# Row factors of two mixing stages spread over partitions through DRAM in place of TensorE transposes, with the planner's ranks set anew

## The chip, the cores and the metric

One core of one Trainium2 chip. The metric is the device time of one execution of the kernel in microseconds, the median of several runs; lower is better.

## The reference

One encoder layer is applied to two independent streams (`x_prompt` and `x_sample`), each 512 tokens of width 1024, everything in float32:

```python
x = x + 0.5 * swiglu(rms_norm(x, ffn1_norm), ...)            # 1024 -> 2816 -> 1024
h = rms_norm(x, mix_norm);  proj = h @ w_in                   # q, k, v, memory q/k/v, gates
att = gqa_block_attention(rope(rms_norm(q)), rope(rms_norm(k)), v)   # 8 heads of 64, softmax over 512 keys
mem = mlstm_bidirectional(...)                                # 4 heads of 128, forward and backward
merged = sigmoid(g_att) * (att @ w_up_att) + sigmoid(g_mlstm) * (mem @ w_up_mlstm)
x = x + merged @ w_out
x = x + 0.5 * swiglu(rms_norm(x, ffn2_norm), ...)
return rms_norm(x, final_norm)
```

Two per-token factors matter here. In the attention each head's output is divided by the sum of its softmax row:

```python
p = softmax(s);  o = p @ v            # the kernel: o = (exp(s - max) @ v) / sum
```

In the memory each head's output is normed over its 128 channels and gated:

```python
h = h * rsqrt(mean(h * h, -1) + EPS) * head_norm
out = sigmoid(o_pre) * h
```

## The kernel before

Activations lie channel-major: 128 channels on the partitions, 512 tokens along the free axis. Matrix products run as pairs of rounded and remaining parts (a weight and an activation are each split into a high and a low part, ACT copies the high part, DVE subtracts it), so a product of 128 channels takes three matmuls of 128x128x512. The two feed-forward parts (to about 640 us, and from about 1440 us) are straight loops. Between them lies the mixing of both streams, and it is the part that is changed.

The mixing isn't written in the order in which it runs. `mix(s, ...)` hands tasks to one planner (class `Plan`), for stream 0 and stream 1 and for parts of what stands before and behind them. Each task has an engine (PE is TensorE, DVE VectorE, ACT ScalarE, SP the queue that issues transfers), a modelled duration, tasks that it depends on, buffers that it takes and frees (`need`, `free`), and a rank. `run()` keeps a modelled clock for each engine and takes, of the tasks that could start at the earliest time, the one with the least rank. The order found so is the order of the instructions on each engine; nothing is reordered on the chip. A product has the base rank 5 (`FILL`), so products that nothing waits for fill gaps of others. The table `RANK` adds a number to the rank of named tasks, "part of the mixing, stream, engine, function"; its entries were found by search. The helper `dma` counts 0.35 us of SP for each transfer, and its landing after the bytes at 400 KB per us and 1.9 us more.

The stages that the change touches, per stream `s`:

- **Attention (`attend`)**. For each head and block of 128 queries, `scores` (two products), `peak` (DVE), `exp` (ACT, which also adds up the row's sum into column `i` of the small tile `tot`, 128 tokens on the partitions x 4 blocks x 2 heads). Then for each block of keys four transposes (`turn`, line 1275), a split (`high` on ACT, `lower` on DVE, line 1284) and `attend` (two products). `copy_o` and `add_o` bring the head's output into one half of the partitions of a tile `af`: two heads of 64 channels fill 128 partitions. The sums lie with tokens on the partitions but are needed along the free axis, repeated over the 64 channels of each head. For that, `recip` takes reciprocals, `spread` (ACT, line 1320) copies them 64 times side by side, `turn_r` (line 1327) turns the result by four 128x128 transposes into a PSUM bank, and `divide` (line 1331) multiplies. A split then writes the `att` tile, which `up_att` (the projection with `w_up_att`) reads. Before it comes `values`, the products that make the memory's values.
- **Memory (`memory`)**, four heads. The head's output stands in a PSUM bank. `squares` (line 1552), four transposes `sums_` (line 1561) and `reduced` make the sum of squares for each token, `rooted` the reciprocal root in eleven small DVE instructions (lines 154 to 172), `cast` spreads it over all partitions by four transposes of a repeated column (`bcast_psum`, line 188), and `ended` (line 1574) multiplies the gated output by it. A split (lines 814 and 817) writes the `mem` tile, which `up_mem` (the projection with `w_up_mlstm`) reads; its products for channel group k depend on head k, four groups to an output bank, nine products for the first three heads and three for the last. Three banks (`mm`) are there for it.

Buffers that play a part: `f2`, two slots of 128 x 2 x 512 numbers, used by `copy_o`, `add_o` (the tile `af`), the first gate of the memory and rows of the output projection; `pt`, two PSUM banks for all transposes; `wr`, four buffers for fetched weights (`fetch_w`, line 198), which ACT (line 830) and DVE (line 833) split.

`bcast_psum` is also used twice in the first feed-forward part (8 of its 40 transposes), which the change doesn't touch.

Of the kernel before, what the change touches and what calls it, by code (L numbers as in the profile page):

```python
# [26 lines left out]
def encoder(ctx, tc, I, outs):  # L27
# [49 lines left out]
    def wide(tag):  # L77
        return tpool.tile([P, 2, S], F32, tag=tag, bufs={"t2": 6, "f2": 2}[tag], name=nm(tag))
# [44 lines left out]
    def PT():  # L123
        return pt.tile([P, S], F32, tag="t", name=nm("pst"))
# [12 lines left out]
    def A(shape, dtype=F32, name="a"):  # L137
        return apool.tile(shape, dtype, tag="a", name=nm(name))
# [45 lines left out]
    def bcast_psum(r, pin=lambda i: i):  # L184

        pr = PT()
        for b in range(4):
            pin(nc.tensor.transpose(pr[:, b * P:(b + 1) * P], r[:, b:b + 1].to_broadcast([P, P]), ident))
        return pr
# [487 lines left out]
    def tok_proj(xh, xl, name, N, kk, done):  # L677
# [6 lines left out]
        def comp(k0, w):  # L684
# [14 lines left out]

    outs_of = []  # L700

    RANK = {"gsums ACT <lambda>": 5, "kv0 ACT raw": 0.5, "kv0 ACT gate": 2.5, "q0 SP w_fetch": -20,
            "rotate0 DVE by_cos": 4, "rotate0 DVE low": 5.5, "mem_qk0 SP w_fetch": -1.5, "mem_qk0 ACT w_high": -8.5,
            "mem_qk0 DVE w_low": 12, "out_gate0 SP w_fetch": -11, "attend0 ACT exp": -3, "attend0 PE turn": -15,
            "attend0 ACT copy_o": 13, "attend0 DVE s_low": 1, "maxima0 DVE masked": 7, "maxima0 DVE peak": 3,
            "maxima0 PE ends": -3, "maxima0 DVE scales": -1, "values0 PE fn": -68, "up_att0 ACT w_high": 14.5,
            "up_att0 PE fn": -2, "memory0 ACT one": 14.5, "memory0 DVE fn": -5, "memory0 PE turn": -1.5,
            "memory0 PE cast": 3.5, "memory0 DVE s_low": 3.5, "up_mem0 DVE w_low": -17, "up_mem0 DVE add": 7,
            "up_mem0 DVE s_low": 0.5, "after0 ACT high": -8, "kv1 ACT w_high": -6, "q1 ACT w_high": -0.5,
            "keys1 ACT copy_k": 18, "rotate1 DVE by_root": 43, "mem_qk1 ACT w_high": 13.5, "mem_qk1 ACT high": 6,  # L710
            "mem_qk1 DVE <lambda>": -6.5, "out_gate1 ACT w_high": -6, "attend1 PE scores": -2.18,
            "attend1 PE turn": -2, "attend1 PE turn_r": -1, "maxima1 DVE peak": -12.5, "values1 PE fn": -11,
            "up_att1 SP w_fetch": 10.5, "up_att1 ACT w_high": 51, "up_att1 PE fn": 9, "up_att1 DVE <lambda>": -15,
            "memory1 DVE masked": 3, "memory1 ACT one": 19, "memory1 ACT high": 27, "memory1 DVE gated": 0.68,
            "memory1 DVE rooted": 9.5, "before1 DVE <lambda>": 13, "up_mem1 PE fn": 13.5, "up_mem1 ACT s_high": 4.5}

    class Plan:

# [77 lines left out]
    def pe(n, width, fn, deps=(), pri=1, need=(), free=()):  # L796
        step = {512: 0.227, 128: 0.109, 16: 0.112}[width]
        return do("PE", n * step, (n - 1) * step + 0.35 + SPARE, fn, deps, pri, need, free)

    def act(w, fn, deps=(), pri=1, need=(), free=(), more=0.0):  # L800
        return do("ACT", ACT_STEP[w] + more, ACT_STEP[w] + 0.12 + more + SPARE, fn, deps, pri, need, free)

    def dve(w, fn, deps=(), pri=1, need=(), free=(), n=1):
        return do("DVE", n * DVE_STEP[w], n * DVE_STEP[w] + 0.08 + SPARE, fn, deps, pri, need, free)
# [16 lines left out]
    def weights(view, deps=(), need=(), w=1024):  # L821
# [15 lines left out]
        t2 = dve(w, w_low, [t1], 2, (), ["wr"])  # L837
        return c, t2

    def unit(c, ready, n, cols, src, done, last=True, each=None):  # L840

        b = {}
        t = None
        for k in range(n):
            for i in range(3):
                def fn(k=k, i=i):
                    if k == 0 and i == 0:
                        b["p"] = MM()
                    sh, sl = src(k)
                    w_, x_ = ((c["hi"], sh), (c["hi"], sl), (c["lo"], sh))[i]  # L850
                    own(nc.tensor.matmul(b["p"], w_[:, k, cols], x_, start=(k == 0 and i == 0),  # L851
                                         stop=(k == n - 1 and i == 2)))
                first, end = k == 0 and i == 0, k == n - 1 and i == 2
                new = [each[k]] if each and i == 0 else []
                t = do("PE", 0.227, 0.35 + SPARE if end else 0.0, fn, new + ([t] if t else ready), FILL, ["mm"] if first else (),
                       ["w"] if end and last else ())
        done(b, t)
        return t

# [33 lines left out]
    def mix(s, before, after, x_in, start, got, more=None):  # L893
# [352 lines left out]
        for h in range(HA):  # L1246
# [66 lines left out]
            if h % 2:  # L1313
                i = h // 2

                def recip(i=i):
                    own(V_.reciprocal(G["tot", i], G["tot", i]))

                def spread(i=i):
                    own(nc.scalar.activation(G["af", i][:, 1].rearrange("p (b i e) -> p b i e", i=2, e=DA),  # L1320
                                             G["tot", i].unsqueeze(3).to_broadcast([P, 4, 2, DA]), AF.Copy))

                def turn_r(i=i):
                    pr = G["rp", i] = PT()
                    for b in range(4):
                        bs = slice(b * P, (b + 1) * P)
                        own(nc.tensor.transpose(pr[:, bs], G["af", i][:, 1, bs], ident))

                def divide(i=i):
                    af = G["af", i][:, 0]  # L1330
                    own(V_.tensor_tensor(af, af, G["rp", i], op=ALU.mult))
                u = dve(8, recip, [exps[g, b] for g in (h - 1, h) for b in range(4)], 1)
                u = act(512, spread, [u, adds[h - 1]], 1)
                u = pe(4, 128, turn_r, [u, last_a[h]], 0, ["pt"])
                u = dve(512, divide, [u, adds[h - 1], adds[h]], 0, (), ["pt"])
                att_in.append(split_of(lambda i=i: G["af", i][:, 0], lambda i=i: att()[:, i, 0, :],
                                       lambda i=i: att()[:, i, 1, :], [u, att_t], 1, free=["f2"]))

# [91 lines left out]
        for h in range(HM):  # L1430
# [136 lines left out]
            def rooted(h=h):  # L1567
                G["rh", h] = rstd_cols(G["cs", h], 4, DM, own)

            def cast(h=h):  # L1570
                G["Rp", h] = bcast_psum(G["rh", h], own)

            def ended(h=h):
                own(V_.scalar_tensor_tensor(ogs[h], ogs[h], hn[:, h:h + 1], G["Rp", h], op0=ALU.mult, op1=ALU.mult))
            sq_ = act(512, squares, [prev], 0, ["turn"])
            gt_ = dve(512, gated, [prev, og_in[h], sq_], 1, (), [bank])
            u = pe(4, 128, sums_, [sq_], 0, ["pt"], ["turn"])
            u = dve(512, reduced, [u], 0, (), ["pt"])
            u = dve(8, rooted, [u], 0, n=20)
            u = pe(4, 128, cast, [u], 0, ["pt"])  # L1580
            u = dve(512, ended, [u, gt_], 0, (), ["pt"])
            mem_in.append(split_of(lambda h=h: ogs[h], lambda h=h: mem()[:, h, 0, :], lambda h=h: mem()[:, h, 1, :],
                                   [u, mem_t], 1))

# [43 lines left out]
        if s:  # L1628
            do.part = f"last{s}"
            swap(w3, ["qk", "qk"], ["w", "w"])  # L1630
            rows, into = {}, [None, None]
            rows_t = do("POOL", 0.0, 0.0, lambda: rows.update(t=A([P, 2, 4, S], F32, "rows")), [mh_t], 0, ["A"])
            ends = []

            def out_last(h):
                def fetch():
                    nc.sync.dma_start(rows["t"][:, h], xbuf[1][:, h])
                into[h] = dma(fetch, [rows_t], 3, kb=1024)

                def done(bk, q, t):  # L1640
                    x = lambda: rows["t"][:, h, q, :]

                    def add():
                        own(V_.scalar_tensor_tensor(x(), bk[q], 0.5, x(), op0=ALU.mult, op1=ALU.add))

                    def sq():
                        own(nc.scalar.activation(bk[q], x(), AF.Square, accum_out=ssq2[1][:, h, q:q + 1]))
                    u = dve(512, add, [t, into[h]], 1)
                    ends.append(act(512, sq, [u], 1, (), [bank_of(q)], more=0.2))
                    dma(lambda: nc.sync.dma_start(x2buf[1][:, h, q, :], x()), [u], 2, kb=256)  # L1650
                return token_blocks([wov[h, j] for j in range(4)], lambda k: (mhl["h"][:, k, :], mhl["l"][:, k, :]), 512, done, [last_w], ended)
            out_t = [out_last(h) for h in range(2)][1]
            swap([out_t], (), ["A", "A"])
            return rows, ends, turned
# [36 lines left out]
    rbuf = [[dpool.tile([P, 7, 2, S], F32, name=f"rbuf{n}_{j}") for j in range(NF // 2)] for n in range(2)]  # L1691
    xnbuf, xn1buf = [dpool.tile([P, KD, S], F32, name=n) for n in ("xnbuf", "xn1buf")]
    gbuf = [[dpool.tile([P, KD, S], F32, name=f"gbuf{s}_{i}") for i in range(2)] for s in range(2)]
    gated_in = [[[], []], [[], []]]
    xc = [None] * 7
    up = Up(xc, I["ffn1_w_gate"], I["ffn1_w_up"], rbuf[0], AHEAD[0])
# [913 lines left out]
```

## Time and profile before

| | |
|---|---|
| median of three runs | 2040.72 us (2040.3 to 2041.28) |
| span of the profiled execution, first to last instruction | 2039.6 us |
| what the runs' median has beyond that span | 1.1 us |
| PE busy | 2021.7 us (99%) |
| DVE busy | 1597.7 us (78%) |
| ACT busy | 965.5 us (47%) |
| granted TensorE clock | 0.999 |

The page gives no time of the profiled execution but its span. Busy times are unions over the span. A group of instructions has a row with its line, engine, operation, tiles and shape, its count, its busy time, the mean duration of one, and the engine's idle time just before it. Matmuls are pipelined: one with 512 columns is recorded as 389 ns long, but the next can start well before that has passed, so the cost of one more is read from start to start. `PEld` is the load of weights, which runs beside products; `SPq` the queue that issues transfers.

### The profile page before, as it was taken

The numbers are of one execution on the slowest core, as the hardware profiler recorded it, in microseconds if no ns is written. First come the engines' busy times: TensorE is split into PE (matmuls) and PEld (weight loads), VectorE is DVE, ScalarE is ACT, GpSimd is POOL, SyncE is SP. The second block draws the span as 40 slices with busy tenths as digits, with TensorE's granted clock in tenths as the row PEclk, the third lists the DMA queues.
The fourth block names the chain that finished last, engine by engine and source line by source line (L and its number), as shares of the span: only waits on it lengthen the run. The fifth ranks groups of instructions, "written<-read, shape, count | busy, mean of one in ns | idle before, by whom it ended". The sixth has DMA issues, their size and how long they took to land.

```text
span 2039.6 us, 26019 instructions
## 1 busy us (share of the span) xinstructions
PE 2021.7 (99%) x9308; PEld 1671.2 (82%) x9308; DVE 1597.7 (78%) x2532; ACT 965.5 (47%) x1604; POOL 23.9 (1%) x49
## 2 busy tenths in 40 slices
PE   9999999999999999999999999999999999999997
PEld 8888888888888888877888888888788888888886
DVE  7997878786796764897888866876888787776687
ACT  7543434342227533587645775656443344343224
POOL 0000000000000000000000000000000000000001
PEclk9999999999999999999999999999999999999999
DMA  9556555799774645312345322464464644389753
GB/s 347 179 174 218 181 191 203 245 363 358 249 252 155 217 150 177 104 42 85 125 133 166 123 83 73 165 208 151 138 230 168 212 173 147 135 303 394 269 201 143
DMA packets 149633, 389.02 MB, mean 191 GB/s; under 512 B 15232, under 2 KB 15296, under 8 KB 147712
## 3 DMA queue, kind: packets, MB, share of 16 engines
q1 hardware_dynamic: 148640, 385.33, 54.5%
q8 instruction: 73, 1.20, 0.2%
q0 software_dynamic: 432, 1.25, 0.2%
q10 hardware_dynamic: 432, 0.79, 0.1%
q14 instruction: 56, 0.46, 0.1%
HBM read 269.31 MB, written 118.00 MB: 190 GB/s over the span
## 4 chain that ended last, share of the span: by engine, by line
PE 89%; DVE 6%; ACT 2%; DMA 1%; issue 1%; SPq 0%; DVEq 0%; ACTq 0%
PE pss L292 17%; PE pst L292 11%; PE mm L851 9%; PE mm L292 8%; PE mm L553 8%; PE mm L881 7%; PE pst L553 4%; PE pss L553 4%; PE pss L2151 3%; PE pso L553 3%; PE mm L2151 2%; PE pso L881 2%; PE pst L2151 2%; PE pst L1275 1%; PE pss L1251 1%
## 5 line engine op out<-in xcount | busy, mean ns | idle before, releaser
L292 PE MATMUL pss<-xc,w 128*128 128x512 f32 x1632 | 389.4, 389 | 1.0 <-ACT w L247 0.6
L292 PEld LDWEIGHTS pss<-xc,w 128*128 128x128 f32 x1632 | 305.9, 188 | 66.2 <-ACT w L247 1.0
L247 ACT ACTIVATE w<-wr 128x1024 fp32r<-128x1024 f32 (+2 forms) x123 | 127.4, 1038 | 219.6 <-PE pst L292 122.9
L248 DVE TENSOR_TENSOR w<-wr,w 128x1024 fp32r<-128x1024 f32 (+2 forms) x123 | 146.9, 1196 | 59.0 <-ACT w L247 58.7
L292 PE MATMUL mm<-xc,w 128*128 128x512 f32 x792 | 190.4, 390 | 0.1
L553 PE MATMUL mm<-w,rt 128*128 128x512 f32 x792 | 185.3, 389 | 0.0
L292 PEld LDWEIGHTS mm<-xc,w 128*128 128x128 f32 x792 | 148.3, 188 | 31.9 <-ACT t L301 0.6
L553 PEld LDWEIGHTS mm<-w,rt 128*128 128x128 f32 x792 | 148.5, 188 | 30.8
L292 PE MATMUL pst<-xc,w 128*128 128x512 f32 x528 | 127.0, 389 | 0.0
L292 PE MATMUL pst<-xc,f 128*128 128x512 f32 x528 | 126.8, 389 | 0.0
L833 DVE TENSOR_TENSOR w<-wr,w 128x1024 fp32r<-128x1024 f32 (+1 forms) x80 | 93.4, 1170 | 35.3 <-ACT w L830 34.9
L292 PEld LDWEIGHTS pst<-xc,w 128*128 128x128 f32 x528 | 99.1, 188 | 20.6
L292 PEld LDWEIGHTS pst<-xc,f 128*128 128x128 f32 x528 | 99.1, 188 | 20.6
L613 ACT ACTIVATE w<-t 128x512 fp32r<-128x512 f32 x82 | 51.5, 631 | 122.0 <-PE pst L553 63.6
L830 ACT ACTIVATE w<-wr 128x1024 fp32r<-128x1024 f32 (+1 forms) x80 | 80.7, 1015 | 56.4 <-PE mm L851 18.9
L613 ACT ACTIVATE w<-wr 128x512 fp32r<-128x512 f32 x72 | 44.7, 631 | 128.6 <-PE pso L553 57.9
L553 PE MATMUL pss<-w,rt 128*128 128x512 f32 x396 | 94.4, 389 | 0.6 <-ACT w L613 0.6
L553 PE MATMUL pst<-w,rt 128*128 128x512 f32 x396 | 94.0, 389 | 0.0
L553 PEld LDWEIGHTS pss<-w,rt 128*128 128x128 f32 x396 | 74.2, 188 | 16.4 <-ACT w L613 1.0
L553 PEld LDWEIGHTS pst<-w,rt 128*128 128x128 f32 x396 | 74.3, 188 | 15.4
L2151 PE MATMUL mm<-xc,w 128*128 128x512 f32 x360 | 83.9, 391 | 1.5 <-ACT f L2181 1.5
L2151 PEld LDWEIGHTS mm<-xc,w 128*128 128x128 f32 x360 | 67.1, 188 | 16.2 <-ACT f L2181 1.9
(403 smaller groups left out, 3878.7 us busy)
## 6 DMA issues: line engine op xcount, KB each, us to landing
rt<-rbuf SPq DMA_DIRECT2D x154, 512.0 KB, 5.7
rbuf<-t SPq DMA_DIRECT2D x72, 512.0 KB, 3.4
wr<-in_ffn_w_gate_dram SPq DMA_DIRECT2D x60, 512.0 KB, 4.4
wr<-in_w_in_cols_dram SPq DMA_DIRECT2D x48, 512.0 KB, 4.3
wr<-in_ffn_w_up_dram SPq DMA_DIRECT2D x44, 512.0 KB, 3.7
rbuf<-f SPq DMA_DIRECT2D x30, 512.0 KB, 3.8
rbuf<-tab SPq DMA_DIRECT2D x30, 512.0 KB, 4.0
wr<-in_ffn_w_down_dram SPq DMA_DIRECT2D x48, 256.0 KB, 6.6
```

Source lines behind the costliest of these rows:

```text
L247: pin(nc.scalar.activation(t[:, 0], src, AF.Copy))
L248: pin(V_.tensor_tensor(t[:, 1], src, f(t[:, 0]), op=ALU.subtract))
L292: pin(nc.tensor.matmul(p, a[:, k, :], xt[:, b, k, :], start=(first and k == 0 and i == 0), stop=(k == HK_ - 1 and i == 2), skip_group_chec ...
L553: nc.tensor.matmul(p, r[:, b, d * P:(d + 1) * P], u[:, a, :], start=(first and q == 0 and k == 0), stop=(q == len(us) - 1 and k == 2), ski ...
L613: nc.scalar.activation(hi, src, AF.Copy)
L830: own(nc.scalar.activation(c["hi"], c["raw"], AF.Copy))
L833: own(V_.tensor_tensor(c["lo"], c["raw"], f(c["hi"]), op=ALU.subtract))
L851: own(nc.tensor.matmul(b["p"], w_[:, k, cols], x_, start=(k == 0 and i == 0), stop=(k == n - 1 and i == 2)))
L881: own(nc.tensor.matmul(b[q][:, :N], x_[:, q * P:(q + 1) * P], w_[:, kl, :], start=(k == 0 and i == 0), stop=(k == KD - 1 and i == 2)))
L1251: own(nc.tensor.matmul(p, G["qT"][:, h, b * P:(b + 1) * P], G["kv"][:, h // 4 * 2 + j, :], start=(j == 0), stop=(j == 1)))
L1275: own(nc.tensor.transpose(p[:, b * P:(b + 1) * P], G["e", h, b // 2][:, b % 2, kb * P:(kb + 1) * P], ident))
L2151: own(nc.tensor.matmul(bank[name], left()[a][:, k, :], xcl[m][:, y, k, :], start=bool(first) and k == 0 and i == 0, stop=(k == HK_ - 1 and ...
```

## The change

In the attention, `spread` and `turn_r` go. `recip` is followed by two transfers that store the reciprocals of the two heads to a DRAM tile `tbuf` (single numbers, 512 for each head), and two that load each head's row of 512 numbers back, repeated over 64 partitions, into the second half of `af`. `divide` reads that half instead of a PSUM bank.

In the memory, `cast` no longer calls `bcast_psum`. `store_h` stores the 512 roots of a head to a DRAM tile `hbuf`, `cast` loads them as a row repeated over 128 partitions into a slot of `f2`, and `ended` reads that slot.

In the output projection of stream 1, a task of the planner that issues no instruction makes the first products wait until the last block of the projections has begun. The entries of `RANK` are replaced by others.

```diff
-    RANK = {"gsums ACT <lambda>": 5, "kv0 ACT raw": 0.5, "kv0 ACT gate": 2.5, "q0 SP w_fetch": -20,
...
-            "memory1 DVE rooted": 9.5, "before1 DVE <lambda>": 13, "up_mem1 PE fn": 13.5, "up_mem1 ACT s_high": 4.5}
+    RANK = {"after1 ACT copy": -18, "attend0 ACT high": -56, "attend0 DVE add_o": 176.5, "attend0 DVE lower": -46.5,
+            "attend0 DVE peak": 30.5, "attend0 DVE recip": 447, "attend0 DVE s_low": 503, "attend0 PE turn": -64,
+            "attend0 SP spread": 85, "attend1 ACT exp": 234, "attend1 DVE add_o": 18, "attend1 DVE divide": -16.5,
...
+            "mem_qk0 ACT w_high": -56.5, "mem_qk0 DVE <lambda>": -239, "mem_qk0 PE fn": 733,
...
+            "up_mem0 DVE s_low": 259.5, "up_mem1 DVE add": 27.5, "up_mem1 PE fn": -88.5, "values0 ACT w_high": -74,
+            "values0 PE fn": -147.5, "values1 ACT s_high": -93.5, "values1 PE fn": -9}
...
+    unit_begun = []
...
+                if first:
+                    unit_begun.append(t)
...
+                def store_r(i=i):
+                    for e in range(2):
+                        nc.sync.dma_start(tbuf[s][i, e].rearrange("(b p) -> p b", p=P), G["tot", i][:, :, e])
+
                 def spread(i=i):
-                    own(nc.scalar.activation(G["af", i][:, 1].rearrange("p (b i e) -> p b i e", i=2, e=DA),
-                                             G["tot", i].unsqueeze(3).to_broadcast([P, 4, 2, DA]), AF.Copy))
-
-                def turn_r(i=i):
-                    pr = G["rp", i] = PT()
-                    for b in range(4):
-                        bs = slice(b * P, (b + 1) * P)
-                        own(nc.tensor.transpose(pr[:, bs], G["af", i][:, 1, bs], ident))
+                    for e in range(2):
+                        nc.sync.dma_start(G["af", i][e * DA:(e + 1) * DA, 1, :], tbuf[s][i, e, :].partition_broadcast(DA))
 
                 def divide(i=i):
                     af = G["af", i][:, 0]
-                    own(V_.tensor_tensor(af, af, G["rp", i], op=ALU.mult))
+                    own(V_.tensor_tensor(af, af, G["af", i][:, 1], op=ALU.mult))
                 u = dve(8, recip, [exps[g, b] for g in (h - 1, h) for b in range(4)], 1)
-                u = act(512, spread, [u, adds[h - 1]], 1)
-                u = pe(4, 128, turn_r, [u, last_a[h]], 0, ["pt"])
-                u = dve(512, divide, [u, adds[h - 1], adds[h]], 0, (), ["pt"])
+                u = dma(store_r, [u], 0, kb=50, n=2)
+                u = dma(spread, [u, adds[h - 1]], 0, kb=256, n=2)
+                u = dve(512, divide, [u, adds[h - 1], adds[h]], 0)
...
+            def store_h(h=h):
+                nc.sync.dma_start(hbuf[s][h].rearrange("(b p) -> p b", p=P), G["rh", h])
+
             def cast(h=h):
-                G["Rp", h] = bcast_psum(G["rh", h], own)
+                G["Rp", h] = wide("f2")
+                nc.sync.dma_start(G["Rp", h][:, 0], hbuf[s][h, :].partition_broadcast(P))
 
             def ended(h=h):
-                own(V_.scalar_tensor_tensor(ogs[h], ogs[h], hn[:, h:h + 1], G["Rp", h], op0=ALU.mult, op1=ALU.mult))
+                own(V_.scalar_tensor_tensor(ogs[h], ogs[h], hn[:, h:h + 1], G["Rp", h][:, 0], op0=ALU.mult, op1=ALU.mult))
...
             u = dve(8, rooted, [u], 0, n=20)
-            u = pe(4, 128, cast, [u], 0, ["pt"])
-            u = dve(512, ended, [u, gt_], 0, (), ["pt"])
+            u = dma(store_h, [u], 0, kb=30)
+            u = dma(cast, [u], 0, ["f2"], kb=256)
+            u = dve(512, ended, [u, gt_], 0, (), ["f2"])
...
+            ended[0] = swap([ended[0], unit_begun[-1]])
...
+    tbuf = [dpool.tile([HA // 2, 2, S], F32, name=f"tbuf{s}") for s in range(2)]
+    hbuf = [dpool.tile([HM, S], F32, name=f"hbuf{s}") for s in range(2)]
```

More of the change, by code (lines that the diff above doesn't have):

```diff
@@ L700, in encoder @@
     outs_of = []
-    RANK = {"gsums ACT <lambda>": 5, "kv0 ACT raw": 0.5, "kv0 ACT gate": 2.5, "q0 SP w_fetch": -20,
[L703 to L714, printed above, removed]
-            "memory1 DVE rooted": 9.5, "before1 DVE <lambda>": 13, "up_mem1 PE fn": 13.5, "up_mem1 ACT s_high": 4.5}
@@ new lines, in encoder @@
+    RANK = {"after1 ACT copy": -18, "attend0 ACT high": -56, "attend0 DVE add_o": 176.5, "attend0 DVE lower": -46.5,
+            "attend0 DVE peak": 30.5, "attend0 DVE recip": 447, "attend0 DVE s_low": 503, "attend0 PE turn": -64,
+            "attend0 SP spread": 85, "attend1 ACT exp": 234, "attend1 DVE add_o": 18, "attend1 DVE divide": -16.5,
+            "attend1 DVE lower": -27.5, "attend1 DVE peak": -13, "attend1 DVE s_low": -64, "attend1 PE scores": 20.5,
+            "attend1 PE turn": 24, "begin ACT out": -74.5, "gates0 DVE <lambda>": -70.5, "grest PE product_": -87.5,
+            "gsums ACT <lambda>": 128, "k0 DVE k_scale": 60, "k1 DVE k_sum": -135, "keys0 PE turn_k": 155.5,
+            "keys1 ACT copy_k": 109, "keys1 PE turn_k": 378.5, "kv1 ACT s_high": -26.5, "kv1 PE fn": -184.5,
+            "kv1 SP w_fetch": -29.5, "maxima0 DVE masked": 145, "maxima0 DVE peak": -40.5, "maxima0 DVE scales": 99.5,
+            "maxima0 PE ends": -173.5, "maxima1 DVE masked": 12.5, "mem_qk0 ACT high": -244.5,
+            "mem_qk0 ACT w_high": -56.5, "mem_qk0 DVE <lambda>": -239, "mem_qk0 PE fn": 733,
+            "mem_qk0 SP w_fetch": -178, "mem_qk1 ACT w_high": 358, "mem_qk1 DVE <lambda>": -56,
+            "mem_qk1 PE fn": 115.5, "memory0 ACT left": -97.5, "memory0 ACT one": 0.5, "memory0 ACT squares": 213,
+            "memory0 DVE fn": -2, "memory0 DVE lower": -2.5, "memory0 DVE masked": 456.5,
+            "memory0 DVE middle": -118.5, "memory0 DVE right": -45, "memory0 PE turn": -67, "memory1 ACT one": -53.5,
+            "memory1 DVE ended": 42, "memory1 DVE gated": 685.5, "memory1 DVE masked": 102, "memory1 DVE rooted": 35,
+            "memory1 DVE s_low": -12.5, "next ACT p_high": 108.5, "out1 ACT w_high": 15, "out_gate0 PE fn": 121,
+            "out_gate1 ACT fn": -125, "out_gate1 PE fn": 404.5, "q0 SP w_fetch": -364.5, "q1 ACT copy": 84,
+            "q1 PE fn": -182, "rotate0 DVE by_root": -2, "rotate1 DVE by_sin": 155.5, "rotate1 DVE low": 111,
+            "rotate1 PE turn_u": 37.5, "up_att0 ACT w_high": -11, "up_att0 DVE w_low": 662, "up_att1 ACT w_high": 391,
[3 rows of a table added]
```

1 row of the table RANK is left out of this document.

## The prediction

> **What bounds the kernel now.** I read the head of the page first, then the busy time in stretches, then what TensorE (PE) waited for.
>
> ```profile
> span 2039.6 us, 26019 instructions
> PE 2021.7 (99%) x9308; PEld 1671.2 (82%) x9308; DVE 1597.7 (78%) x2532; ACT 965.5 (47%) x1604; POOL 23.9 (1%) x49
> ```
> ```profile
> 640.00:1440.00 800.00, 795.15 (x3893) 657.64 (x3892) 606.34 (x1134) 468.96 (x888) 2.66 (x20) 1.00 0.42 136
> ...
> 840.00:880.00 40.00, 39.01 (x188) 31.04 (x187) 38.64 (x77) 21.40 (x41) 0.00 (x0) 1.00 0.31 81
> 880.00:940.00 60.00, 59.99 (x324) 49.15 (x323) 55.20 (x99) 52.12 (x119) 0.00 (x0) 1.00 0.13 36
> ```
> ```profile
> PE mm L2151 <- ACT f L2181: 1.5, 1, 1.5
> ```
>
> In the stretches the columns after the length are PE, weight loads, DVE, ACT and POOL, then granted clock, DMA share and GB/s. The planned mixing lies in 640 to 1440 us: PE is busy 795.15 of 800.00 us there at a granted clock of 1.00, idle 4.85 us, and its longest single wait is 1.5 us. So one PE instruction less is time off the end, as long as nothing new makes PE stand; and no more than 4.85 us can be had there by ordering alone. DVE is at 606.34 of 800 over the whole, but at 38.64 of 40 where the first attention starts and at 55.20 of 60 in its body. That is where a worse order could show.
>
> **The change part by part.** *Transposes removed.* They are in the groups of instructions, with the mixing's share of the broadcast helper (line 188) taken from 640 to 1440 us:
>
> ```profile
> L1327 PE MATMUL pst<-ident,f 128*128 128x128 f32 x32 | 4.9, 274 | 0.0
> L188 PE MATMUL pst<-ident,rs 128*128 128x128 f32 x32 | 4.6, 272 | 0.0
> ```
>
> The busy time of these, 9.5 us, overlaps the neighbouring products, so I price a group of four from start to start, in the timeline of PE:
>
> ```profile
> 967.30 4.25 PE L851 MATMUL mm<-xc,w 128*128 128x512 f32 x18
> 971.39 0.60 PE L188 MATMUL pst<-ident,rs 128*128 128x128 f32 x4
> 971.74 3.68 PE L851 MATMUL mm<-xc,w 128*128 128x512 f32 x15
> 975.26 0.93 PE L1526 MATMUL pst<-ident,t 128*128 128x128 f32 x7
> ```
>
> 18 products take 971.39 - 967.30 = 4.09 us, 0.227 each. The four transposes take 0.35 us, and the 15 products behind them 3.52 instead of 15 x 0.227 = 3.41, so a group costs 0.35 + 0.09 to 0.11, some 0.44 us. There are 64/4 = 16 groups (one per head pair and stream, one per memory head and stream): 16 x 0.44 = 7.0 us off PE. Bounds: 16 x 0.35 = 5.6 and the full busy time, 9.5.
>
> *ACT and DVE.* The spreading copy on ACT goes; the multiplications of DVE stay and read SBUF instead of PSUM.
>
> ```profile
> L1320 ACT ACTIVATE f<-tot 128x512 f32<-128x512 f32 x8 | 5.0, 626 | 0.1
> ```
>
> 5.0 us leave ACT, which has 331 us idle in the mixing: nothing on the path. `divide` and `ended` I leave at their present duration.
>
> *Transfers added.* Per head pair two stores of 512 numbers and two loads that repeat a row over 64 partitions; per memory head one store and one load over 128 partitions. That is 8 x 4 + 8 x 2 = 48 issues on SP. Nearest rows of the DMA issues (the last number is us from issue to landing):
>
> ```profile
> box<-ebuf SPq DMA_DIRECT2D x32, 256.0 KB, 4.5
> ...
> ebuf<-er SPq DMA_DIRECT2D x2, 16.0 KB, 1.6
> g<-in_ffn_norm_dram SPq DMA_DIRECT2D x1, 4.0 KB, 4.2
> ...
> hn<-in_mlstm_head_norm_dram SPq DMA_DIRECT2D x1, 2.0 KB, 2.5
> ```
>
> The load is the shape of the box loads, 4.5 us. The store writes single numbers, which no row shows. Lower bound 1.6 us (a small store in whole rows). For the upper one I take the slowest load of 128 short runs, 4.2 us, and count what it has over 1.6 four times, for 512 runs: 1.6 + 4 x 2.6 = 12 us. I take 3 us, near the 2.5 of the smallest load. The chain from a root to the spread row is then 3 + 4.5 = 7.5 us, where a transpose group took 0.4; 6 us at best, 16.5 at worst.
>
> The Trainium skill speaks against such a store: its page "DMA: Bandwidth & Descriptors", section "Rules for kernel authors", says that a non-contiguous last dimension becomes one descriptor per element, and its section "Bandwidth" gives about 10.5 ns per packet beside a fixed 2.0 us. By that, as an estimate, 512 descriptors make 2.0 + 5.4 = 7.4 us for the store and 11.9 for the chain. No run shown here has such a store.
>
> *Where the chain is covered.* For the softmax sums the cover already stands there: the attention's products end before 940 us (the stretch above) in the first stream, and the first product that reads the divided rows starts at 997.3, behind the products of the values; the second stream has the same stages.
>
> ```profile
> L851 PE MATMUL mm<-att,w x192: 387/389/477, 997.3 to 1324.2; 128*128 128x512 f32 x192
> ```
>
> The new ranks put the first stream's reciprocals and splits far behind DVE's other work (447 and 503), which these 57 us also hold. Were this cover gone, the last pair of each stream would cost PE up to 7.5 us. For the memory only the last head of each stream counts. First stream: the root is done at 1026.4 us.
>
> ```profile
> 1026.22 0.16 DVE L167 SCALAR_TENSOR_TENSOR rs<-rs,rs 128x4 f32<-128x4 f32 x1
> ```
> ```profile
> L1574 DVE SCALAR_TENSOR_TENSOR box<-box,hn,pst x8: 736/741/748, 972.2 to 1324.5; 128x512 f32<-128x512 f32 x8
> ```
> ```profile
> L814 ACT ACTIVATE mem<-box x8: 615/627/635, 973.3 to 1325.8; 128x512 fp32r<-128x512 f32 x8
> L817 DVE TENSOR_TENSOR mem<-box,mem x8: 681/686/692, 976.1 to 1327.0; 128x512 fp32r<-128x512 f32 x8
> ```
> ```profile
> 1031.79 4.58 PE L851 MATMUL mm<-mem,w 128*128 128x512 f32 x19
> ```
>
> The chain gives 1033.9, and multiply and split (0.74 + 0.63 + 0.69 us) 1036.0. The projection of the memory begins at 1031.79 and has three banks of nine products before it needs this head, to 1031.79 + 27 x 0.227 = 1037.9: covered. Second stream:
>
> ```profile
> 1318.21 1.21 DVE L833 TENSOR_TENSOR w<-wr,w 128x1024 fp32r<-128x1024 f32 x1
> ...
> 1323.08 0.16 DVE L167 SCALAR_TENSOR_TENSOR rs<-rs,rs 128x4 f32<-128x4 f32 x1
> ```
> ```profile
> 1312.94 0.60 PE L188 MATMUL pst<-ident,rs 128*128 128x128 f32 x4
> ...
> 1316.94 7.10 PE L851 MATMUL mm<-att,w 128*128 128x512 f32 x30
> 1323.87 0.60 PE L188 MATMUL pst<-ident,rs 128*128 128x128 f32 x4
> ...
> 1324.54 0.63 PE L851 MATMUL mm<-mem,w 128*128 128x512 f32 x2
> ```
>
> Root done 1323.24, rows ready 1323.24 + 7.5 + 2.06 = 1332.8; needed at 1324.1 (the transposes gone) + 27 x 0.227 = 1330.2: 2.6 us of standing if the order stays. But of the 5.0 us from 1318.21 to 1323.24 only 2.2 are the root's eleven small steps (0.2 apart), the rest is other work of DVE ahead of it, and the 30 products on PE do not depend on the chain; the planner, which counts 2.3 + 2.9 us for the two transfers, can move either. I take 0 and keep 2.6; with a 12 us store it is 11.6.
>
> *SP's queue.* The second transfer waits on SP until the first has landed, and weight fetches stand behind it.
>
> ```profile
> SPq L198 <- DVE w L833: 303.8, 64, 19.4
> ```
> ```profile
> ACT w L830 <- DMA wr<-in_w_in_mv_dram: 4.0, 1, 4.0
> ```
>
> SP itself stood 303.8 us for free weight buffers, and the longest that ACT waited there for a weight fetch was 4.0 us, once. With four buffers of 24 products (5.4 us each), a fetch has 21.8 us less a landing as of the box loads, 4.5, and the split (1.21 on DVE, as much on ACT): about 15 us to spare. The planner counts 2.3 us for a store, so a store of 3 holds SP 0.7 us, and even one of 12 us holds it 10: nothing. With the spare gone, 0.7 us would reach PE up to 16 times, 11 us.
>
> *The rest.* The loaded row takes one of two `f2` slots for 4.5 + 0.74 us per memory head, with the other held by the first gate; the last two heads, the closest, come 10.9 us apart (1312.94 and 1323.87 above), so nothing. The wait put on the last output projection is an order for the planner, without an instruction: nothing. The new ranks move every engine's order: between -4.85 us (all present standing gone) and a loss that the last rival bounds; I take 0, as the stages' work is otherwise the same.
>
> Sum: 2039.6 - 7.0 = 2032.6 for the span. The page gives the execution's span only; the runs' median, 2040.72, is 1.1 above it. So **2033.6 us**.
>
> **The rivals.** *Standing goes too.* The searched order removes most of the 4.85 us: 2033.6 - 4 = 2029.6. For: the longest wait, 1.5 us, is an ordering matter. Against: it lies outside the changed part.
>
> *The store is slow and the second stream's end waits.* With a store in the middle of its bounds, 7 us, the rows are ready at 1336.8, PE stands 6.6 us, and the time is 2040.2, no change; with 12 us, 2045. For: no row shows single-number stores. Against: the 30 free products. By the Trainium skill's packet figure on the same page the standing would be 7.0 us.
>
> *SP blocks the weights*: decides only where its holds pass the 15 us of spare, hence a store over some 17 us, or several holds in one block of weights; the 11 us above make 2044.8, the edge of slower.
>
> *The filler is spent early (slower).* The attention alone keeps DVE longer than PE:
>
> ```profile
> L1284 DVE TENSOR_TENSOR t<-pst,t 128x512 fp32r<-128x512 f32 x64 | 43.3, 683 | 4.2 <-ACT t L1280 3.9
> L1256 DVE TENSOR_REDUCE asm<-pss 128x1 f32<-128x512 f32 x64 | 43.3, 681 | 7.2 <-PE pss L1251 6.6
> ```
>
> Per head DVE has 4 x 0.683 + 4 x 0.681, one addition of about the same and half a division and split, 0.68 each: 6.8 us. PE has 16 long products of 0.227 and 16 transposes of 0.11: 5.4. Without other products PE stands 1.4 us a head, 23 us over 16 heads; it begins where fewer than 6 filler products per head are left. If the new ranks spend them too early for half the heads, 2033.6 + 8 x 1.4 = 2044.8, and for all 2056; the time passes the old one from five heads on. For: DVE at 38.64 of 40. Against: PE stands 0.01 us in 880 to 940 now.
>
> **How the numbers follow.** Less than 0.2% (4.1 us) is what a measurement of this kernel can hardly tell from no change. My forecast (2030.5 to 2036.6) 0.55; standing gone as well 0.15; late end 0.15 (0.02 of it still faster, 0.13 the same); filler spent 0.12 (0.02 same, 0.10 slower); SP blocked 0.03 (0.01 same, 0.02 slower). Faster 0.72, same 0.16, slower 0.12. From 2028.5 to 2043 some 0.8 is held: below lies part of the second case, above most of the last two.
>
> **What would show it.** Right: 64 transposes fewer on PE, PE busy in the mixing down by 7 to 9.5 us, idle still near 5; stores landing in 2 to 4 us; no wait of PE on `ended` or `divide`. Wrong: PE products of the memory projection waiting for the split of the last head (late store), weight splits on ACT waiting for fetches (SP), or PE's scores and attention products waiting for DVE around 860 to 940 and 1120 to 1210 us (filler).

## The result, and the profile after

The changed kernel takes 2138.05 us in the median of four runs (2137.01 to 2141.28), the kernel before 2041.0 in runs beside it: a ratio of 1.0477, interval [1.0463, 1.0492]. That is 97 us slower, where 2033.6 was forecast and 2043 was the end of the range. The busy times and the stretches of the profiled execution (span 2139.5 us) answer to those shown of before:

```profile
PE 2044.2 (96%) x9244; PEld 1684.1 (79%) x9244; DVE 1600.5 (75%) x2532; ACT 961.7 (45%) x1596; POOL 26.4 (1%) x49
```
```profile
640.00:1440.00 800.00, 719.59 (x3370) 589.19 (x3369) 539.50 (x1045) 404.65 (x791) 3.66 (x20) 0.94 0.41 116
1440.00:1540.00 100.00, 99.96 (x473) 83.07 (x472) 70.75 (x92) 60.73 (x92) 0.00 (x0) 1.00 0.62 202
```

The 64 transposes are gone: 9244 matmuls, not 9308. The planned products now run from 643.2 to 1535.9 us, 892.7 us where they took 795.2 (642.4 to 1437.6), so nearly the whole loss lies there: 97.5 of the 99.9 us by which the span grew. In 640 to 1540 us PE is idle 900 - 719.59 - 99.96 = 80.4 us where it had been idle 4.85 in 640 to 1440, and its granted clock in 640 to 1440 is 0.94 where it was 1.00. PE's busy time in these stretches, 819.55 us, is 24.4 above the 795.15 of before, with 64 transposes fewer. Only some 2.5 us of that are products that lie outside the planned ones: the same work also ran slower.

The waits of DVE, ACT and PE, from three lists (us in total, times, longest us), show who stood:

```profile
DVE box L1588 <- DMA f<-hbuf: 69.7, 8, 10.1
DVE f L1341 <- DMA f<-tbuf: 21.5, 7, 5.6
```
```profile
ACT mem L822 <- DVE box L1588: 88.4, 8, 17.6
```
```profile
PE pss L1477 <- DVE t L1486: 18.0, 2, 9.1
PE pst L1571 <- ACT t L1562: 16.5, 2, 8.2
PE mm L861 <- ACT mem L822: 11.9, 2, 7.8
PE pso L1302 <- DVE t L1296: 9.5, 3, 5.0
PE pst L1287 <- DVE t L1296: 7.6, 2, 5.3
PE pss L1477 <- DVE qk L1216: 7.0, 1, 7.0
```

`ended` (now line 1588) waits for its row at all eight heads, 8.7 us each, and `divide` (1341) at seven of eight pairs: 91.2 us in which DVE does nothing. No row of PE names the transfers. Most of what PE waits for are inputs of scores, turns and sums of squares, made by DVE and ACT, that need no row from DRAM; only 11.9 us are the memory's projection waiting for a split of `mem`. The DMA issues say why (KB each, us from issue to landing):

```profile
f<-tbuf SPq DMA_DIRECT2D x16, 128.0 KB, 4.3
f<-hbuf SPq DMA_DIRECT2D x8, 256.0 KB, 4.2
...
tbuf<-tot SPq DMA_DIRECT2D x16, 2.0 KB, 9.2
...
hbuf<-rs SPq DMA_DIRECT2D x8, 2.0 KB, 10.2
...
ebuf<-er SPq DMA_DIRECT2D x2, 16.0 KB, 1.4
```

These are medians. The loads take what was forecast, 4.2 and 4.3 us. The stores of 2 KB take 9.2 and 10.2 us, three times what I took, and a store of 16 KB in whole rows 1.4. One head in the timelines of SP, DVE and PE shows how that reaches PE:

```profile
984.90 0.37 SPq L1581 DMA_DIRECT2D hbuf<-rs  x1
995.13 0.32 SPq L1585 DMA_DIRECT2D f<-hbuf  x1
```
```profile
989.97 0.69 DVE L1544 TENSOR_TENSOR t<-pst,t 128x512 fp32r<-128x512 f32 x1 [0.43 <-ACT t L1540]
999.39 0.75 DVE L1588 SCALAR_TENSOR_TENSOR box<-box,hn,f 128x512 f32<-128x512 f32 x1 [8.73 <-DMA f<-hbuf]
1000.06 0.68 DVE L1216 TENSOR_TENSOR qk<-mm,qk 128x512 fp32r<-128x512 f32 x1
```
```profile
993.45 0.39 PE L1477 MATMUL pss<-qk 128*128 128x512 f32 x1
1000.80 2.50 PE L1477 MATMUL pss<-qk 128*128 128x512 f32 x5 [6.96 <-DVE qk L1216]
1003.10 1.91 PE L861 MATMUL mm<-xc,w 128*128 128x512 f32 x4
```

The store is issued at 984.90 and has landed at 995.13; the load follows at once and is there at 999.39. DVE has finished its earlier work at 990.66 and stands 8.73 us at `ended`. Behind `ended` in DVE's queue is the low part of `qk` for the *next* head, 0.68 us of work with its inputs ready (ACT had made the high part by 992.2), and PE, which has come in its own order to a product that reads it, stands 6.96 us for it. Then the first five products take 1003.10 - 1000.80 = 2.30 us, 0.46 each, twice the 0.227 of before: the granted clock has fallen. In three stretches of 12 us from there on the column after POOL gives it:

```profile
1000.00:1012.00 12.00, 11.20 (x38) 8.98 (x39) 9.39 (x31) 7.43 (x21) 0.00 (x0) 0.71 0.30 91
1012.00:1024.00 12.00, 12.00 (x62) 10.11 (x61) 8.07 (x21) 6.71 (x14) 0.00 (x0) 1.00 0.79 143
1024.00:1036.00 12.00, 3.01 (x9) 2.15 (x8) 4.54 (x12) 4.14 (x14) 0.00 (x0) 0.65 0.42 142
```

The Trainium skill has this in "TensorE: Matmul & The Clock Gate", Part 1: an idle window of about 3.4 us halves the clock until PE has been busy about as long again. The trace agrees on the halving: 0.46 us for a product after 6.96 us of standing, and 1.00 in the stretch without a stand. The way back took longer than that here: the granted clock is 0.50 from 1000.8 to 1006.9 us, 6.1 us of busy PE, and 0.99 from there to 1012.

This one head stands for all. PE has 13 stands of over 1 us in the mixing, 76.0 us together, and each ends 1.3 to 4.5 us after DVE has gone on at `ended` (eight of them) or at `divide` (five).

From the starts of all planned matmuls the 97.5 come to two parts. Where more than 0.5 us passes from one start to the next, what goes beyond a product's 0.227 is 88.9 us against 6.2 before: +82.6. All other time between starts grows by 14.9, although the transposes are gone from it. At their forecast price of 7.0 us, the products that ran slow cost some 22.

### The profile page after: what moved, and what is told of

It is laid out like the page before. It is cut to its first block, busy times and chain, and to the rows that moved or that the text cites. A ratio compares the mean times of both kernels' runs of the same rounds, so it can differ in the third digit from the quotient of the medians.

```text
span 2139.5 us, 25968 instructions
## 1 busy us (share of the span) xinstructions
PE 2044.2 (96%) x9244; PEld 1684.1 (79%) x9244; DVE 1600.5 (75%) x2532; ACT 961.7 (45%) x1596; POOL 26.4 (1%) x49
## 4 chain that ended last, share of the span: by engine, by line
PE 74%; DMA 11%; DVE 10%; ACT 3%; issue 2%; SPq 0%; DVEq 0%; ACTq 0%
PE pss L292 16%; PE pst L292 10%; PE mm L553 8%; PE mm L292 7%; PE mm L893 7%; PE pst L553 4%; PE pss L553 4%; DMA hbuf<-rs 4%; PE mm L861 3%; PE pss L2169 3%; DMA tbuf<-tot 3%; PE pso L553 2%; PE mm L2169 2%; PE pso L893 2%; PE pst L2169 2%
```

## The experiments

Three causes stood against each other: the slow store, the new ranks, and the transfers as such (the round trip and SP's queue, whatever the store takes).

**The ranks of before.** The changed kernel, with the old table `RANK`:

```diff
-    RANK = {"after1 ACT copy": -18, "attend0 ACT high": -56, ...
+    RANK = {"gsums ACT <lambda>": 5, "kv0 ACT raw": 0.5, ...
```

> The transfers as in the changed kernel, with the ranks of the kernel before. Theory W (waiting): the stores of single numbers land 9 to 10 us after issue where the planner counts 2.3, and DVE, which works in order, stands at the multiplication behind them (91 us in the changed kernel); the ranks only decide how much of it shows. Expected: DVE again stands 50 to 100 us at the two multiplications, 2090 to 2140 us. Rival R (ranks): the new order loses the time by itself, and the transfers are covered: 2030 to 2041 us, little standing at the multiplications.

Measured 2155.8 us, ratio 1.056 [1.0542, 1.0578], 18 us above the changed kernel and above the range that I had given. The stores landed in 8.7 and 9.8 us, and DVE stood at the same places, 73.1 us in all, at `ended` for example:

```profile
DVE box L1580 <- DMA f<-hbuf: 54.1, 8, 10.8
```

So the loss doesn't need the new ranks; with the transfers they are worth 18 us. The other corner, transposes under the new ranks, has no time: the planner finds no complete order with them. The wait put on the last output projection is in every kernel with transfers and was not tried alone.

**Stores in runs of four.** The same numbers, in another order in DRAM: each partition writes its four numbers side by side, 128 runs of 16 bytes in place of 512 single numbers, and the two multiplications read the row with a step of four. The planner's tasks and durations are untouched, so every engine has the same order.

```diff
-  nc.sync.dma_start(hbuf[s][h].rearrange("(b p) -> p b", p=P), G["rh", h])
+  nc.sync.dma_start(hbuf[s][h].rearrange("(p b) -> p b", b=4), G["rh", h])
...
-  own(V_.scalar_tensor_tensor(ogs[h], ogs[h], hn[:, h:h + 1], G["Rp", h][:, 0], op0=ALU.mult, op1=ALU.mult))
+  o = ogs[h].rearrange("q (b p) -> q b p", b=4)
+  own(V_.scalar_tensor_tensor(o, o, hn[:, h:h + 1], G["Rp", h][:, 0].rearrange("q (p b) -> q b p", b=4),
+                              op0=ALU.mult, op1=ALU.mult))
```

(and `store_r`, `tot` and `divide` in the same way)

> The changed kernel, with the four numbers of a partition side by side in DRAM: a store writes 128 runs of 16 bytes instead of 512 of 4, and the multiplications read the row in that order. Theory W with a landing that goes by the count of runs: the landing beyond about 1.6 us falls to a quarter, to some 4 us, DVE's standing to a third of 91 us, the time to 2060 to 2080 us. Theory W with a landing that goes by the bytes of a line that many small writes share: 16-byte runs still share lines, landing 6 to 10 us, 2100 to 2140 us. Rival R: unchanged, 2130 to 2145 us.

Measured 2047.32 us, ratio 1.003 [1.0019, 1.0042]: 91 of the 97 us are gone with the order unchanged, more than I had expected, as the stores land in 2.1 us and not in 4. Its landings, DVE's waits for `hbuf`'s rows, and the mixing:

```profile
f<-tbuf SPq DMA_DIRECT2D x16, 128.0 KB, 2.9
f<-hbuf SPq DMA_DIRECT2D x8, 256.0 KB, 4.9
...
tbuf<-tot SPq DMA_DIRECT2D x16, 2.0 KB, 2.1
...
hbuf<-rs SPq DMA_DIRECT2D x8, 2.0 KB, 2.1
```
```profile
DVE box L1590 <- DMA f<-hbuf: 10.7, 7, 2.9
```
```profile
640.00:1440.00 800.00, 789.31 (x3814) 650.79 (x3813) 607.97 (x1129) 460.82 (x878) 3.66 (x20) 1.00 0.44 140
```

With the store at 2.1 us DVE's wait for `hbuf`'s rows falls from 69.7 to 10.7 us, the one for `tbuf`'s is gone, the clock is 1.00 again and PE's idle time in 640 to 1440 is 10.7 us. This is the cause of the loss in this order: the time of the store. SP's queue and the round trip as such are left with the 6 us that remain, and those have a share of the edit in them, since the step of four makes `ended` 1.13 us long in place of 0.75 and `divide` 1.08 in place of 0.69.

**The memory's stores alone in runs of four.** The same edit for `hbuf` and `ended` only.

> The changed kernel, its order of instructions kept, with runs of four numbers in the stores of the memory's roots alone; the softmax sums keep their stores of single numbers. Theory W: of the 91 us that DVE stands, the memory's 70 go (to about 11, as with runs of four in both), the attention's 21 stay, and the time is 2047 + 20 to 30 us, 2065 to 2080. If the attention's stores cost more than DVE's standing at their division shows (their slow landings also hold SP): above 2085. If they are covered, as the prediction had it: 2047 to 2055.

Measured 2064.24 us, ratio 1.0113 [1.0096, 1.0129], just below the range. The memory's eight stores carry 2138.05 - 2064.24 = 74 us, the softmax sums' sixteen the other 17, in which DVE still stood:

```profile
DVE f L1341 <- DMA f<-tbuf: 18.8, 6, 5.4
```

**What makes the store slow.** Two kernels add to the kernel before, behind its last output, a chain of single stores, each waiting for the one ahead; nothing else runs then. The first varies count and distance, the second the distance in steps and the order in time.

```diff
+    for kind in ("first", "single", "near", "far", "one", "two", "sixteen", "rows", "full", "again"):
...
+        else:
+            pin(nc.sync.dma_start(src[0:1, 0:1], last[0:1].rearrange("(a b) -> a b", a=1)))
+        last = dpool.tile([512 * 128], F32, name=f"z_{kind}")
+        pin(nc.sync.dma_start(*store_of(src, last, kind)))
```

> The kernel before, with single stores in a chain behind its last output, each issued after the one before has landed and been read: 512 single numbers side by side, the same 64 and 512 bytes apart, 128 and 256 single numbers side by side, 128 runs of 16 bytes, 4 rows of 512 bytes, 128 rows of 2048 bytes, and the 512 side by side again. The time is that of the kernel before plus 60 to 120 us and only the landings count. If the landing goes by the count of runs: 512 near 10 us in all three spacings, 256 near 6, 128 near 4, also with 16 bytes; 4 rows 1.5. If it goes by the line that small writes share: 10 us side by side, near 2.5 with 512 bytes between. If neither (a wait behind other transfers): all of them 1.5 to 3 us here, where nothing else runs.

> The kernel before with a second chain of single stores behind its last output, all of 512 single numbers: side by side in the order of the change, 8, 16, 32 and 64 bytes apart in that order, and side by side in the order that gives a partition's four numbers neighbouring places. Side by side should land in 8 to 10 us and 64 bytes apart in 1.9 us again. If the slow landing comes of several numbers in one piece of 64 bytes: 8, 16 and 32 bytes apart fall in steps between 9 and 2 us, and the last is as slow as the first, since 16 numbers share such a piece there too. If it comes of pieces shared by several partitions far from each other in the order of the transfer: the last lands in 2 to 3 us, though it has as many single numbers.

The stores' landings, first kernel and second:

```profile
z_single<-m_single SPq DMA_DIRECT2D x1, 2.0 KB, 8.5
...
z_near<-m_near SPq DMA_DIRECT2D x1, 2.0 KB, 1.9
...
z_one<-m_one SPq DMA_DIRECT2D x1, 0.5 KB, 7.4
...
z_sixteen<-m_sixteen SPq DMA_DIRECT2D x1, 2.0 KB, 2.2
```
```profile
z_single<-m_single SPq DMA_DIRECT2D x1, 2.0 KB, 8.9
...
z_pairs<-m_pairs SPq DMA_DIRECT2D x1, 2.0 KB, 4.5
...
z_fours<-m_fours SPq DMA_DIRECT2D x1, 2.0 KB, 2.7
...
z_eights<-m_eights SPq DMA_DIRECT2D x1, 2.0 KB, 2.0
...
z_quad<-m_quad SPq DMA_DIRECT2D x1, 2.0 KB, 8.5
...
z_single_more<-m_single_more SPq DMA_DIRECT2D x1, 2.0 KB, 8.6
```

It isn't the count: 512 single numbers, each 64 bytes from the next (`near`), land in 1.9 us, while 128 side by side (`one`) take 7.4 and 256 (`two`) 10.2. Nor is it the place in the sequence (8.9 and 8.6 us, second and seventh store of their kernel), nor that neighbouring numbers come from different partitions (`quad`: four neighbouring numbers by one partition, still written one by one, 8.5). What counts is how close the single writes stand: side by side 8.5 to 8.9 us, 8 bytes apart 4.5, 16 apart 2.7, 32 apart 2.0, 64 apart 1.9 and 2.0. The time isn't spent in sending, either: in the trace of the first kernel the packets of 4 bytes are all through 1.3 us after the issue, in `single` as in `near`, and what differs is how long the landing takes after them. Writes that share a short piece of memory and wait there for one another would give all this, but that is an argument: the runs show the distances alone, and not how long such a piece would be.

The Trainium skill's estimate for the store, 7.4 us by "DMA: Bandwidth & Descriptors", section "Bandwidth" (its fixed 2.0 us stand in the section "Anatomy of one DMA"), was the best figure on hand and near the 8.5. The mechanism behind it isn't what the runs show: its time per packet would be the same for `near`, which took 1.9 us.

**The slow store, known to the planner.** The single-number stores stay; the planner is told of 8.0 us more for each store and 1.5 for each load (`late`), and the ranks are searched anew on its clock.

```diff
-            u = dma(store_h, [u], 0, kb=30)
-            u = dma(cast, [u], 0, ["f2"], kb=256)
+            u = dma(store_h, [u], 0, kb=30, late=8.0)
+            u = dma(cast, [u], 0, ["f2"], kb=256, late=1.5)
```

> The changed kernel with its slow stores of single numbers as they are, but the planner is told their landing: 8 us more for a store and 1.5 us more for a load, and the ranks are searched anew against the planner's own clock, which then ends 13.7 us later than for the kernel before. Theory W (DVE is given the multiplication too early and stands at it, with everything behind it): stores still land in 9 to 10 us, but DVE's standing at the two multiplications falls from 91 us to below 25, and the time to 2050 to 2070 us. Rival S (the slow store costs the time itself, through SP or the DMA queues, whatever the order): 2110 us or more, though DVE stands less.

Measured 2066.16 us, ratio 1.0117 [1.0102, 1.0133], with stores of 10.0 and 9.6 us, and with DVE's waits for rows down to this one (besides 4.5 us in which it waited for the store itself to free its source):

```profile
tbuf<-tot SPq DMA_DIRECT2D x16, 2.0 KB, 10.0
...
hbuf<-rs SPq DMA_DIRECT2D x8, 2.0 KB, 9.6
```
```profile
DVE box L1567 <- DMA f<-hbuf: 8.2, 2, 5.3
```

So 72 of the 97 us go away with the store as long as it was, once the order counts on it: the planner had counted 5.2 us from the root to the row, which came after some 14. The other 25 stay in the best order that my search found for the long store; a better one may exist.

**The fast store, known to the planner; and the transposes with ranks searched as long.** Three kernels on ranks from the same search. The first has stores in runs of four for both stages and tells the planner their times and those of the slower multiplications; the second has them for the attention alone and keeps the memory's transposes; the third is the kernel before, with new ranks only.

```diff
-            u = dma(store_h, [u], 0, kb=30)
-            u = dma(cast, [u], 0, ["f2"], kb=256)
-            u = dve(512, ended, [u, gt_], 0, (), ["f2"])
+            u = dma(store_h, [u], 0, kb=30, late=0.8)
+            u = dma(cast, [u], 0, ["f2"], kb=256, late=2.0)
+            u = dve(512, ended, [u, gt_], 0, (), ["f2"], n=2)
```

> Runs of four numbers in all stores, and the planner told what they cost: 0.8 us more for a store and 2 us more for a load than it counted, 1.2 us for the two multiplications; ranks searched anew against its own clock, which ends 4.1 us before that of the kernel before. Theory W (what is left over the forecast with runs of four is the chain's remaining lateness against the plan): DVE stands below 5 us at the two multiplications, the time is 2036 to 2039 us, faster than before by 0.1 to 0.25%. Rival S (transfers cost the mixing something that the plan doesn't have, such as slower weight fetches): 2041 to 2048 us, with little standing of DVE at the multiplications.

> The softmax sums go through DRAM in runs of four, the memory's roots by transposes as before; the planner is told 0.8 and 1.5 us more for the transfers, ranks searched anew, its clock ends 1.7 us before that of the kernel before. Eight groups of transposes gone are worth 3.5 us. If the attention's chain is covered, as the prediction had it: no standing of DVE at the division, 2037 to 2040 us. If not: 2042 us or more, with standing at the division.

> The kernel before, unchanged but for ranks searched anew in the same way and for as long; the planner's clock ends 1.5 us earlier. It tells what the search alone gives: 2039 to 2042 us. If the search overfits the planner's model, slower than before, 2043 us or more; then the other two have to be read against this one.

| kernel | median us | ratio to before |
|---|---|---|
| fast store, both stages | 2037.44 (2036.82 to 2040.95) | 0.9986 [0.9977, 0.9994] |
| fast store, attention alone | 2043.16 (2040.53 to 2045.99) | 1.0011 [1.0002, 1.002] |
| transposes, ranks searched | 2045.6 (2043.8 to 2048.09) | 1.0022 [1.0013, 1.0031] |

The first is the one version with a median below that of the kernel before, by 3.35 us or 0.14%, which is inside the 0.2% that I called hard to tell from no change. Its only wait for a row, and its mixing:

```profile
DVE box L1569 <- DMA f<-hbuf: 0.6, 1, 0.6
```
```profile
640.00:1440.00 800.00, 793.27 (x3850) 655.22 (x3849) 614.12 (x1137) 464.90 (x883) 3.68 (x20) 1.00 0.43 142
```

On ranks from the same search, transfers against transposes is 2037.44 - 2045.6 = -8.2 us, and the planned products take 790.3 us against 798.0, -7.7. The forecast price of the transposes was 7.0, between 5.6 and 9.5. That the search alone made the kernel 4.8 us slower, although the planner's own clock had put it 1.5 us ahead, shows how far that clock is to be trusted: a few us of these differences are the order's. The second kernel shows it too: DVE never stands at `divide` there, so the attention's chain is covered, and yet the time is not the 2037 to 2040 us that I had expected of that case. For this reason the split between the stages, -2.4 for the attention and -5.7 for the memory, where eight groups each would give 3.5, is open; the ranges of the second and third kernel overlap.

## Why the prediction was wrong, step by step

**PE as the bound, and the price of the transposes: right.** Between the two kernels on ranks from the same search the transposes are worth 7.7 to 8.2 us, with a few us of the order in that; leaving out the gaps of over 0.5 us between starts, as above, the planned products take 6.9 us less. In the changed kernel itself the price can't be told from the slow products.

**The store: mis-sized.** This term, "I take 3 us, near the 2.5 of the smallest load", is the first that failed. It measured 9.2 and 10.2 us, inside the bounds of 1.6 to 12. I chose the value by the nearest row, which was a load; nothing in the rows spoke for a store of single numbers to be near it. The load, 4.5, was right: 4.2 and 4.3.

**The cover: this is the step that turned a small error into 97 us.** "For the memory only the last head of each stream counts" asked only when PE needs the factor. Put the measured chain of 14.4 us into that working, and the last heads give (14.4 - 7.5) + 2.6 = 9.5 us of standing in the second stream and 1026.4 + 14.4 + 2.06 - 1037.9 = 5.0 in the first; measured are 7.8 and 4.1, the two waits of the memory's projection for `mem`, together the 11.9 us above. So far the rival of the late end holds, with its price. The other 64.1 of the 76.0 us in PE's 13 long stands came by a way that was not in the text: `ended` and `divide` are instructions in DVE's queue, at the place where a planner counting 2.3 + 2.9 us put them, and everything behind them on DVE waits too. I had asked who needs the row, not what is queued behind the instruction that waits for it. DVE stood at eight heads of eight. The attention, where I called the cover safe until 997, shows the same at 932.97 us, on DVE and then on PE:

```profile
932.97 0.69 DVE L1341 TENSOR_TENSOR f<-f 128x512 f32<-128x512 f32 x1 [5.62 <-DMA f<-tbuf]
```
```profile
934.32 1.12 PE L1287 MATMUL pst<-ident,t 128*128 128x128 f32 x4 [5.29 <-DVE t L1296]
```

No product needs that divided tile yet, but the split of the next turns stands behind it. ACT, with the high part of `mem` in its own order, stood 88.4 us behind DVE, and PE was left without scores, turns and sums.

**The clock.** It was no term of the sum. PE had not stood longer than 1.5 us before, so its price could not be seen there; it added some 22 us.

**SP's queue: right.** SP did stand for the stores, but ACT waited no more than before for a weight fetch in the mixing (once, 3.5 us, where it had been 4.0), as the spare of 15 us said:

```profile
SPq L198 <- DVE w L841: 221.2, 56, 18.6
SPq L1337 <- DMA tbuf<-tot: 74.5, 13, 10.7
SPq L1585 <- DMA hbuf<-rs: 70.9, 8, 10.9
```

SP waited 145.4 us for the stores, and its waits for free weight buffers fell from 303.8 to 221.2 us, by 82.6. So over half of the hold seems to have fallen into time in which SP would have stood anyway.

**The ranks, taken at 0: neither cause nor nothing.** With the transfers in place they gave 18 us (2155.8 against 2138.05). The filler spent early, the slower rival, is not the cause either, though PE did wait for DVE in the attention (9.5 and 7.6 us in the list of PE's waits): in the kernel with runs of four, whose order is the same, those two waits are gone but for 0.2 us each, and PE's longest in the mixing is this:

```profile
PE pss L1478 <- DVE t L1487: 3.4, 2, 2.2
```

## What to carry to other kernels

Where a step with a known short duration is replaced by one of unknown length, price it twice: for the engine that needs the result, and for the engine that must wait for it in order, with all that is queued behind the wait. If the order is made from a model of durations, the model's figure for the new step is itself a term of the sum: here being wrong about the store cost 72 us, and its length itself at most 25, in the best order found for it. And before numbers go to DRAM singly, look at how they lie there: the same 512 numbers took 2.1 us in runs of four, and 9 to 10 as single numbers side by side.

## What the runs showed of the hardware

- A store's landing time can be set by the distance of its writes in DRAM, not by their number or bytes. Single 4-byte writes side by side land late, 512 of them in 8.5 to 8.9 us, 256 in 10.2 and 128 in 7.4, while 512 that stand 32 or 64 bytes apart land in 1.9 to 2.0 and 128 runs of 16 bytes in 2.2. The packets were through 1.3 us after the issue in the slow store and in the fast one.
- After a stand of 7 us PE's first products took 0.46 us in place of 0.227, at a granted clock of 0.50 for 6.1 us; 82.6 us of standing cost some 22 more in this way.
- DVE reading a 128x512 float32 row with a step of four numbers took 1.08 and 1.13 us where the plain reading took 0.69 and 0.75 (a product of two tiles, and the product with a scalar per partition).
